# Weight loads of the down projection's block products issued four units ahead instead of five

## The chip, the cores and the metric

The kernel runs on one core of a Trainium2 chip. The metric is the device time of one execution in microseconds (us). The kernel before takes 2042.51 us, the median of three runs (2041.34 to 2043.54). The engines are TensorE (PE; its weight loads are PEld), VectorE (DVE), ScalarE (ACT), GpSimd (POOL) and SyncE (SP), which issues most DMAs.

## The reference

The program is a two-layer decoder trunk over 512 tokens of width 1024. Each layer is a SwiGLU FFN, a token mixer (a gated DeltaNet in layer 0, spatial gating in layer 1) and another FFN; so there are four FFNs. Only the FFN's last matrix product is touched by the change:

```
def swiglu(h, w_gate, w_up, w_down):
    return (jax.nn.silu(h @ w_gate) * (h @ w_up)) @ w_down      # D_FF = 2816, D_MODEL = 1024
x = x + 0.5 * rmsnorm(swiglu(rmsnorm(x, g0), w_gate, w_up, w_down), g1)
```

## The kernel before, in words

**Split operands.** Every fp32 operand is split into a rounded high part and a low part (`split`, line 106: a cast on ACT at L108, a subtraction on DVE at L110), and a product is three matmuls: high by high, high by low, low by high. A loaded weight tile thus costs one DMA on SP's queue, one ACT cast and one DVE subtraction.

**The down projection** (`down`, line 536) multiplies the gated activations (22 row blocks of 128, `m` before the split, `ms` after it) by `w_down`. Its result lies in eight PSUM banks `y`, two for each of the blocks (1,0), (0,0), (1,1) and (0,1). Row blocks 0 to 7 are not multiplied plainly: they are taken as a 2x2 block matrix in a scheme with seven products instead of eight. Its products are named a11, s1, s2, a12, s3, a22 and s4. Each has two halves (q = 0, 1), and each half needs a weight tile `dw` (24 matmuls of 512 columns per product); the first half brings the activations `dm` too. For s1, s2, a12 and s3 VectorE first builds sums of weight blocks (`dsum`) or of activations (`dts`). `load_down` (line 472) issues all of that: the DMAs into `raw` (a ring of four buffers), the sums, the casts and the subtractions.

**One bank, several products.** a11, s2, s3 and a22 add up in the same two banks, block (1,0). After a11, after s2 and after s3 the running sum has to be kept: `keep` (line 574) copies both banks to a tile `dk` on ACT (L579). The next product of that block adds to the same banks, so TensorE may not begin it before the copy.

**The order of the work.** `ORDER` interleaves the products with four plain row blocks (8 to 11), whose matmuls go to the blocks (0,0) and (1,1) first:

```
ORDER = ("a11", 8, "s1", 9, "s2", 10, "a12", 11, "s3", "a22", "s4")
def ahead(self, n):
    while sum(c for _, c in self.ready) < n and self.queue:
        load, cost = self.queue.pop(0)
        self.ready.append((load(), cost))

def wget(self, n=1):
    self.ahead(n)
    out = [self.ready.pop(0)[0] for _ in range(n)]
    self.ahead(self.depth)
    return out
```

A unit is one half of a product or one plain row block. `wget` hands out the next unit and then issues loads until `depth` units stand ready, before the matmuls of the unit that it handed out are written. `depth` is 3 in the rest of the kernel. `need` (line 700) splits the activations of the plain row blocks into `ms` when their turn comes. A scheduler then orders each engine's instructions and may move an instruction past others that it thinks not ready; each engine works its own list in order. Between the a11 halves stand two leftover steps of the gate and up projections (`pa`, `pc`, L400), the last of which is `p3`.

Of the kernel before, what the change touches and what calls it, by code (L numbers as in the profile page):

```python
# [27 lines left out]
class Trunk:  # L28
# [507 lines left out]
    def down(self, get, need, on_token, rest):  # L536

        nc = self.nc
        V = nc.vector
        d = {}  # L540
        for blk in ((1, 0), (0, 0), (1, 1), (0, 1)):
            d[blk] = [self.bank("y") for _ in range(2)]
        begun = set()
        rest = list(rest)

        def mm(blk, s, lhsT, rhs, stop=False):
            nc.tensor.matmul(d[blk][s], lhsT, rhs, start=(blk, s) not in begun, stop=stop, skip_group_check=True)  # L547
            begun.add((blk, s))

        def product(blk):  # L550
            m = None
            for q in range(2):
                (w, mq), = self.wget()
                m = mq or m
                for s in range(2):
                    for j in range(2):
                        l = [m[:, i, q * 2 + j, s * P:(s + 1) * P] for i in range(2)]
                        for a, b in ((0, 0), (0, 1), (1, 0)):
                            mm(blk, s, l[a], w[:, b, j])
                if rest:  # L560
                    rest.pop(0)()
            self.tick()

        def plain(kt, wt, blks, stop=False):
            for blk in blks:
                i, k = blk
                for s in range(2):
                    m = get(kt, 2 * k + s)
                    for a, b in ((0, 0), (0, 1), (1, 0)):
                        mm(blk, s, m[a], wt[b][:, i * 512:(i + 1) * 512], stop and a == 1)  # L570

        keeps = {}

        def keep(blk, n):
            if n != 2:
                keeps["t"] = self.big([P, 2, 2, 512], F32, name="dk")
            k = keeps[n] = keeps["t"][:, 0 if n != 2 else 1]
            for s in range(2):
                nc.scalar.copy(out=k[:, s], in_=d[blk][s])  # L579

        def add(out, blk, k):
            for s in range(2):
                V.tensor_tensor(out=d[blk][s] if out is None else out[:, s], in0=d[blk][s], in1=k[:, s], op=ALU.add)

        self.depth = 5
        held = []
        for n in self.ORDER:
            if isinstance(n, int):
                need(n)
                wt, = self.wget()  # L590
                plain(n, wt, ((0, 0), (1, 1)))
                held.append((n, wt))
                self.tick()
                continue
            if n == "s3":
                add(None, (0, 0), keeps[1])
            product({"a12": (0, 0), "s1": (0, 1), "s4": (0, 1)}.get(n, (1, 0)))
            if n in ("a11", "s2", "s3"):
                keep((1, 0), {"a11": 1, "s2": 2, "s3": 3}[n])
            if n == "s3":  # L600
                add(keeps[3], (0, 1), keeps[3])
                add(None, (1, 1), keeps[3])
        self.depth = 3
        on_token.prepare()
        add(None, (0, 1), keeps[2])
        for blk in ((1, 0), (0, 1)):
            for kt, wt in held:
                plain(kt, wt, (blk,))
            self.tick()
        for kt in range(12, NF - 5):  # L610
            need(kt)
            wt, = self.wget()
            plain(kt, wt, ((0, 0), (1, 0), (0, 1), (1, 1)))
            self.tick()
        need(NF - 1)
        tail = self.wget(5)
        for t in range(NT):
            for hfs in (((0, 1),) if t < NT - 1 else ((0,), (1,))):
                for i, kt in enumerate(range(NF - 5, NF)):
                    m = get(kt, t)  # L620
                    for a, b in ((0, 0), (0, 1), (1, 0)):
                        for hf in hfs:
                            mm((hf, t // 2), t % 2, m[a], tail[i][b][:, hf * 512:(hf + 1) * 512], kt == NF - 1 and a == 1)
                    if i == 1 and hfs[0] == 0:
                        self.tick()
            on_token(t, d[(0, t // 2)][t % 2], d[(1, t // 2)][t % 2])
            self.tick()
# [1008 lines left out]
```

## Time and profile before

| | us |
|---|---|
| median of three runs | 2042.51 |
| the profiled execution | 2040.34 |
| its span, first to last instruction | 2038.6 |
| TensorE busy in it | 1986.3 |
| TensorE idle until a `dk` copy, four times | 21.0 |
| mean granted TensorE clock | 0.992 of full speed |

The profile is one execution. The span is what lies between the first and the last instruction, and 1.74 us lie around it. TensorE is busy for 97% of it, so a reader looks for the stretches in which it isn't, or in which its clock is lower. The four down projections begin at 247, 925, 1275 and 1906 us.

### The profile page before, as it was taken

How to read it: one execution, taken by the hardware profiler on the slowest of the kernel's cores; microseconds unless marked ns; L12 is line 12 of the kernel's file. 1: busy time of each engine (PE TensorE's matmuls, PEld its weight loads, DVE VectorE, ACT ScalarE, POOL GpSimd, SP SyncE). 2: the span in 40 equal slices, each digit the busy share in tenths (PEclk: the TensorE clock that was granted, in tenths of full speed). 3: DMA queues.
4: the chain of work that ended last, by engine and by line, in shares of the span. 5: the costliest groups of instructions: out<-in, count | busy, mean ns of one | idle time of the engine just before them, and what ended most of it. 6: DMA issues, size and time to landing. Idle time of an engine off the chain costs nothing.

```text
span 2038.6 us, 32697 instructions
## 1 busy us (share of the span) xinstructions
PE 1986.3 (97%) x13418; PEld 1804.3 (89%) x13418; DVE 1436.0 (70%) x2006; ACT 966.4 (47%) x1688; POOL 131.6 (6%) x202
## 2 busy tenths in 40 slices
PE   7999989999998999998999999899999999999898
PEld 7999978988877899997889999788888889999887
DVE  6787793777946688888568887947455529888862
ACT  5455552585435555555345555534223426555451
POOL 1000000111135100000010000001000000000000
PEclk9999999999999999999999999999999999999999
DMA  5333364244221433335522333553322613333451
GB/s 166 94 111 107 117 204 145 85 142 125 92 74 68 141 94 104 108 112 183 208 73 90 110 113 115 181 196 133 99 84 83 228 51 96 112 102 106 153 188 42
DMA packets 172424, 246.45 MB, mean 121 GB/s; under 512 B 19257, under 2 KB 131185, under 8 KB 169842
## 3 DMA queue, kind: packets, MB, share of 16 engines
q1 hardware_dynamic: 162946, 212.68, 33.7%
q10 hardware_dynamic: 9328, 31.68, 4.0%
q8 instruction: 105, 1.72, 0.4%
q14 instruction: 45, 0.37, 0.1%
HBM read 230.12 MB, written 14.21 MB: 120 GB/s over the span
## 4 chain that ended last, share of the span: by engine, by line
PE 63%; DVE 3%; issue 1%; ACT 1%; POOL 0%; DMA 0%; ACTq 0%; DVEq 0%; POOLq 0%
PE pa L400 17%; PE y L547 15%; PE pc L400 8%; PE y L334 6%; PE pb L400 4%; PE pu L201 2%; PE pu L200 2%; PE pu L199 2%; PE pv L199 1%; PE pv L201 1%; PE pv L200 1%; PE px L1467 1%; DVE dw L110 1%; PE pg L200 0%; PE pg L201 0%
## 5 line engine op out<-in xcount | busy, mean ns | idle before, releaser
L547 PE MATMUL y<-w,ms 128*128 128x512 f32 x1344 | 315.7, 395 | 0.0
L547 PEld LDWEIGHTS y<-w,ms 128*128 128x128 f32 x1344 | 255.6, 191 | 54.6 <-DVE ms L110 1.5
L400 PE MATMUL pa<-hsh,ws 128*128 128x256 f32 x1248 | 250.1, 283 | 0.0
L108 ACT CAST ws<-wsum 128x1024 fp32r<-128x1024 f32 x156 | 161.8, 1051 | 117.8 <-DVE wsum L170 100.8
L400 PEld LDWEIGHTS pa<-hsh,ws 128*128 128x128 f32 x1248 | 206.1, 192 | 0.0
L110 DVE TENSOR_TENSOR w<-raw,w 128x1024 fp32r<-128x1024 f32 x154 | 186.0, 1225 | 24.7 <-ACT w L108 23.9
L110 DVE TENSOR_TENSOR ws<-wsum,ws 128x1024 fp32r<-128x1024 f32 x156 | 189.5, 1222 | 10.6 <-ACT ws L108 9.2
L547 PE MATMUL y<-dw,dm 128*128 128x512 f32 x672 | 161.2, 396 | 21.1 <-ACT dk L579 21.0
L108 ACT CAST w<-raw 128x1024 fp32r<-128x1024 f32 x155 | 158.5, 1049 | 40.8 <-DMA raw<-in_sg_w_out 6.7
L400 PE MATMUL pa<-hsl,ws 128*128 128x256 f32 x624 | 176.9, 283 | 0.0
L547 PEld LDWEIGHTS y<-dw,dm 128*128 128x128 f32 x672 | 126.5, 190 | 49.5 <-ACT dk L579 22.3
L408 ACT COPY keep<-pa 128x256 f32<-128x256 f32 x234 | 86.5, 370 | 146.5 <-PE pa L400 144.2
L311 DVE TENSOR_TENSOR bt<-y,gain 128x512 f32<-128x512 f32 x48 | 32.7, 689 | 156.0 <-ACT junk L307 155.5
L400 PE MATMUL pa<-hq,wa 128*128 128x256 f32 x936 | 125.4, 283 | 0.0
L400 PE MATMUL pb<-hq,wa 128*128 128x256 f32 x936 | 125.1, 283 | 0.0
L400 PE MATMUL pc<-hsh,ws 128*128 128x256 f32 x624 | 125.1, 283 | 0.0
L400 PE MATMUL pa<-hsh,wd 128*128 128x256 f32 x624 | 125.0, 283 | 0.0
L400 PE MATMUL pc<-hq,ws 128*128 128x256 f32 x936 | 125.0, 283 | 0.0
L400 PEld LDWEIGHTS pa<-hsl,ws 128*128 128x128 f32 x624 | 119.9, 192 | 0.0
L400 PEld LDWEIGHTS pc<-hq,ws 128*128 128x128 f32 x936 | 118.2, 192 | 0.3
L400 PEld LDWEIGHTS pa<-hq,wa 128*128 128x128 f32 x936 | 118.1, 192 | 0.0
L400 PEld LDWEIGHTS pb<-hq,wa 128*128 128x128 f32 x936 | 118.0, 192 | 0.0
(328 smaller groups left out, 4306.7 us busy)
## 6 DMA issues: line engine op xcount, KB each, us to landing
raw<-in_ffn_w_down SPq DMA_DIRECT2D x120, 512.0 KB, 4.3
raw<-in_ffn_w_gate SPq DMA_DIRECT2D x88, 512.0 KB, 3.8
raw<-in_ffn_w_up SPq DMA_DIRECT2D x88, 512.0 KB, 4.1
raw<-in_dn_w_in SPq DMA_DIRECT2D x32, 512.0 KB, 4.5
raw<-in_sg_w_in SPq DMA_DIRECT2D x32, 512.0 KB, 4.4
xs<-x ACTq DMA_DIRECT2D x20, 512.0 KB, 2.6
x<-xs ACTq DMA_DIRECT2D x10, 1024.0 KB, 10.1
raw<-in_sg_w_out SPq DMA_DIRECT2D x16, 512.0 KB, 4.5
```

The lines of the kernel that those rows point to most:

```text
L108: self.nc.scalar.copy(out=hi, in_=src)
L110: e.tensor_tensor(out=lo, in0=src, in1=hi.bitcast(F32), op=ALU.subtract)
L199: nc.tensor.matmul(out, lhsT[0], rhs[0], start=start, stop=False)
L200: nc.tensor.matmul(out, lhsT[0], rhs[1], start=False, stop=False)
L201: nc.tensor.matmul(out, lhsT[1], rhs[0], start=False, stop=stop)
L311: nc.vector.tensor_tensor(out=tmp[:, c], in0=y, in1=grow[:, c], op=ALU.mult)
L334: self.nc.tensor.matmul(y[t][hf], m[a], wt[b][:, hf * 512:(hf + 1) * 512], start=(kt == 0 and a == 0 and b == 0), stop=(kt == nk - 1 and a ...
L400: nc.tensor.matmul(out, wts[w][x][:, k], t[y][:, k], start=(first and k == 0 and m == 0), stop=(k == 3 and m == 2), skip_group_check=not f ...
L408: nc.scalar.copy(out=kept[n], in_=ba)
L547: nc.tensor.matmul(d[blk][s], lhsT, rhs, start=(blk, s) not in begun, stop=stop, skip_group_check=True)
L1467: nc.tensor.matmul(px[:, n * P:(n + 1) * P], self.v[c // 4][:, n, c % 4 * P:(c % 4 + 1) * P], self.wt[:, cp], start=True, stop=True)
```

## The change

The number of units that stand ready ahead while the block products run becomes four. Nothing else is edited.

```
@@ -582,7 +582,7 @@
             for s in range(2):
                 V.tensor_tensor(out=d[blk][s] if out is None else out[:, s], in0=d[blk][s], in1=k[:, s], op=ALU.add)
 
-        self.depth = 5
+        self.depth = 4
         held = []
         for n in self.ORDER:
             if isinstance(n, int):
```

Before, when the second half of a11 was handed out, the first half of s2 (five units on) was loaded at once, ahead of the copies that follow a11. Now the loads then stop at row block 9, and the first half of s2 is loaded when row block 8 is handed out, after `need(8)`.

On ACT, in the fourth down projection, from the cast of row block 9's weights to the second `ms` cast, this stood before (`dk_18877` is the copy after a11, `y_18783` and `y_18784` are the banks of block (1,0), `dw_18844` and `dm_18848` belong to s2, `ms_18880` to row block 8):

```order
L108 CAST w_18813<-raw_18811 128x1024 [waits DMAHW3_49]
L108 CAST dw_18844<-dsum_18664 128x1024 [waits DVE_49,PE_49]
L108 CAST dm_18848<-dts_18670 128x1024 [waits DVE_49,PE_49]
L579 COPY dk_18877<-y_18783 128x512 [waits PE_49]
L579 COPY dk_18877<-y_18784 128x512 [waits PE_49]
L108 CAST ms_18880<-m_17053 128x1024
L108 CAST ms_18883<-m_17053 128x1024
```

and this stands now (`dk_18867` is the copy, `ms_18870` row block 8, `dw_18879` and `dm_18883` s2):

```order
L108 CAST w_18838<-raw_18836 128x1024 [waits DMAHW3_49]
L579 COPY dk_18867<-y_18783 128x512 [waits PE_49]
L579 COPY dk_18867<-y_18784 128x512 [waits PE_49]
L108 CAST ms_18870<-m_17053 128x1024
L108 CAST ms_18873<-m_17053 128x1024
L108 CAST dw_18879<-dsum_18664 128x1024 [waits DVE_49]
L108 CAST dm_18883<-dts_18670 128x1024 [waits DVE_49]
```

The two casts of s2 have moved from before the copies to behind the two `ms` casts. On TensorE, at the same place, from p3 (`pc`) to the first matmuls of s1 (`dw_18796`), this stood before:

```order
L400 MATMUL pc_18699<-hq_15845,ws_18560 128x256 x12
L547 MATMUL y_18783<-dw_18844,dm_18848 128x512 x3
L547 MATMUL y_18785<-w_18681,ms_18880 128x512 x2
L547 MATMUL y_18786<-w_18681,ms_18880 128x512
L547 MATMUL y_18785<-w_18681,ms_18880 128x512
L547 MATMUL y_18786<-w_18681,ms_18880 128x512 x2
L547 MATMUL y_18787<-w_18681,ms_18880 128x512 x3
L547 MATMUL y_18788<-w_18681,ms_18880 128x512 x3
L547 MATMUL y_18789<-dw_18796,dm_18800 128x512 x6
```

and this stands now:

```order
L400 MATMUL pc_18699<-hq_15845,ws_18560 128x256 x12
L547 MATMUL y_18785<-w_18681,ms_18870 128x512 x2
L547 MATMUL y_18786<-w_18681,ms_18870 128x512 x2
L547 MATMUL y_18787<-w_18681,ms_18870 128x512 x2
L547 MATMUL y_18788<-w_18681,ms_18870 128x512 x2
L547 MATMUL y_18785<-w_18681,ms_18870 128x512
L547 MATMUL y_18786<-w_18681,ms_18870 128x512
L547 MATMUL y_18787<-w_18681,ms_18870 128x512
L547 MATMUL y_18788<-w_18681,ms_18870 128x512
L547 MATMUL y_18789<-dw_18796,dm_18800 128x512 x6
```

Three matmuls of s2 stood in front of row block 8; they are gone from there and stand with the other 21 of s2, behind row block 9. At the copies after s3 ACT had this before (`dw_19084` is the last half of s4, `w_19101` row block 12):

```order
L108 CAST dw_19084<-dsum_18664 128x1024 [waits DVE_49]
L108 CAST w_19101<-raw_19099 128x1024 [waits DMAHW0_49,PE_49]
L579 COPY dk_19116<-y_18783 128x512 [waits DVE_49,PE_49]
L579 COPY dk_19116<-y_18784 128x512 [waits PE_49]
L108 CAST w_19125<-raw_19123 128x1024
```

and has this now (`dw_19096` is the last half of s4, `w_19120` row block 12):

```order
L108 CAST dw_19096<-dsum_18664 128x1024 [waits DVE_49]
L579 COPY dk_19111<-y_18783 128x512 [waits PE_49]
L579 COPY dk_19111<-y_18784 128x512
L108 CAST w_19120<-raw_19118 128x1024 [waits DMAHW0_49]
```

The copies now precede row block 12's cast, and the second copy has no wait of its own any more: the first copy's wait on TensorE covers both banks. The order of the DMAs on SP's queue is the same in both programs.

## Rows read from the trace of the kernel before

**Rows 1.** The page: the span, and TensorE's share of it.
```profile
span 2038.6 us, 32697 instructions
PE 1986.3 (97%) x13418; PEld 1804.3 (89%) x13418; DVE 1436.0 (70%) x2006; ACT 966.4 (47%) x1688; POOL 131.6 (6%) x202
```

**Rows 2.** Waits of TensorE: us in total, times, longest us.
```profile
PE y L547 <- ACT dk L579: 21.0, 4, 5.2
```

**Rows 3.** Timeline, TensorE, fourth projection: start, us, what [idle before <-releaser].
```profile
1913.38 1.59 PE L400 MATMUL pc<-hq,ws 128*128 128x256 f32 x12
1920.22 1.78 PE L547 MATMUL y<-dw,dm 128*128 128x512 f32 x3 [5.25 <-ACT dk L579]
1921.80 4.93 PE L547 MATMUL y<-w,ms 128*128 128x512 f32 x12
1926.57 5.63 PE L547 MATMUL y<-dw,dm 128*128 128x512 f32 x24
...
1950.39 16.48 PE L547 MATMUL y<-dw,dm 128*128 128x512 f32 x72
1966.71 65.44 PE L547 MATMUL y<-w,ms 128*128 128x512 f32 x288
```

**Rows 4.** Timeline, TensorE, the same place in down projections one to three.
```profile
260.82 1.78 PE L547 MATMUL y<-dw,dm 128*128 128x512 f32 x3 [5.25 <-ACT dk L579]
...
265.86 5.61 PE L547 MATMUL y<-dw,dm 128*128 128x512 f32 x24
...
938.30 1.78 PE L547 MATMUL y<-dw,dm 128*128 128x512 f32 x3 [5.25 <-ACT dk L579]
...
944.15 5.62 PE L547 MATMUL y<-dw,dm 128*128 128x512 f32 x24
...
1289.13 1.78 PE L547 MATMUL y<-dw,dm 128*128 128x512 f32 x3 [5.24 <-ACT dk L579]
...
1295.32 5.61 PE L547 MATMUL y<-dw,dm 128*128 128x512 f32 x24
```

**Rows 5.** Timeline, ACT, the same place in the fourth down projection.
```profile
1913.35 1.04 ACT L108 CAST w<-raw 128x1024 fp32r<-128x1024 f32 x1
...
1917.50 1.04 ACT L108 CAST dw<-dsum 128x1024 fp32r<-128x1024 f32 x1 [3.11 <-DVE dsum L494]
...
1919.59 1.07 ACT L579 COPY dk<-y 128x512 f32<-128x512 f32 x2
...
1920.54 2.00 ACT L108 CAST ms<-m 128x1024 fp32r<-128x1024 f32 x2
```

**Rows 6.** Busy time by stretch: A:B, us, engines, granted clock, DMA share, GB/s.
```profile
1919.00:1920.00 1.00, 0.00 (x0) 0.00 (x0) 1.00 (x2) 1.00 (x2) 0.00 (x0) 0.65 0.71 227
...
1925.50:1926.00 0.50, 0.50 (x2) 0.40 (x2) 0.50 (x1) 0.50 (x1) 0.00 (x0) 0.50 0.00 0
```

**Rows 7.** Timeline, DVE, fourth down projection: bank additions and subtractions that follow each other.
```profile
1952.04 1.29 DVE L583 TENSOR_TENSOR y<-y,dk 128x512 f32<-128x512 f32 x2
...
1959.34 3.48 DVE L110 TENSOR_TENSOR w<-raw,w 128x1024 fp32r<-128x1024 f32 x3
```

**Rows 8.** Timeline, DVE, second down projection, the sum for s3's second half.
```profile
960.06 1.23 DVE L501 TENSOR_TENSOR raw<-raw,raw 128x1024 f32<-128x1024 f32 x1 [1.94 <-DMA raw<-in_ffn_w_down]
```

**Rows 9.** Timeline, ACT, the copies after s3 in the fourth down projection.
```profile
1954.67 0.59 ACT L579 COPY dk<-y 128x512 f32<-128x512 f32 x1 [0.30 <-PE y L547]
1956.03 0.59 ACT L579 COPY dk<-y 128x512 f32<-128x512 f32 x1 [0.77 <-PE y L547]
```

**Rows 10.** Timeline, TensorE, two other waits, in the DeltaNet.
```profile
597.86 4.75 PE L1220 MATMUL pw<-ninv,kb 128*128 128x128 f32 x24 [2.31 <-DVE kb L1216]
...
649.01 1.09 PE L1293 MATMUL po<-vn,ea 64*64 64x128 f32 x16 [1.54 <-DVE vn L1275]
```

**Rows 11.** Busy time by stretch around the waits of the group above.
```profile
645.00:650.00 5.00, 3.46 (x40) 2.54 (x34) 3.92 (x5) 0.28 (x1) 1.61 (x1) 1.00 1.00 372
...
598.00:602.00 4.00, 3.94 (x20) 3.68 (x21) 2.71 (x2) 0.97 (x2) 4.00 (x4) 0.57 0.29 114
```

More of the change, by code (lines that the diff above doesn't have):

```diff
@@ L583, in add @@
                 V.tensor_tensor(out=d[blk][s] if out is None else out[:, s], in0=d[blk][s], in1=k[:, s], op=ALU.add)
-        self.depth = 5
+        self.depth = 4
         held = []
```

## The prediction

> **What bounds the kernel now.** I read the page first: TensorE is busy for 1986.3 of 2038.6 us [rows 1], so only its idle time, or time at a lower clock, can be won. The waits of TensorE come next. One kind stands out: four waits for a `dk` copy on ACT, 21.0 us in all, 5.2 us the longest [rows 2]. One lies in each down projection, at the same place: before three matmuls of s2, which need the copy after a11 [rows 3, 4]. Then the timeline of ACT at that place, to see why the copy is late. p3 ends on TensorE at 1913.38 + 1.59 = 1914.97 [rows 3] and a11 before it, so the copy could have begun then. ACT, however, works its list in order, and before the copies stand the casts of s2's first half. The first of them idles 3.11 us until VectorE has built the sum, at 1917.50; the copies begin only at 1919.59 [rows 5]. Last, the granted clock: it is 0.65 between 1919 and 1920 and still 0.50 (1.2 GHz) just before 1926 [rows 6], after TensorE had done nothing from 1914.97 to 1920.22. So the matmuls behind the wait pay too: row block 8's 12 take 4.93 us, where 72 in a row take 1966.71 - 1950.39 = 16.32 us, or 0.227 each [rows 3].
>
> The place as a whole, from the end of p3 to the start of s1, is 1926.57 - 1914.97 = 11.60 us in the fourth projection [rows 3]. In the others the end of p3 is the start of the three matmuls less their wait [rows 4]: 265.86 - 255.57 = 10.29, 944.15 - 933.05 = 11.10, and 1295.32 - 1283.89 = 11.43.
>
> **The change, part by part.** *Moved: the load of s2's first half.* It is one DMA, two VectorE sums (`dsum`, `dts`), two ACT casts and two VectorE subtractions, now written behind the copies and behind the casts for row block 8. SP's order is the same in both programs, and its DMA waits for a free buffer of the ring, so it is issued as before. No work is removed or added; what changes is who stands before whom.
>
> *The new place on ACT.* Row block 9's cast ends at 1913.35 + 1.04 = 1914.39. The copy pair takes 1920.54 - 1919.59 = 0.95 us of ACT's list, one `ms` cast about 1.05 (two took 2.00) [rows 5], so the high part of `ms` is there at 1916.39. In the trace the first matmul came 0.2 us after that cast (1920.54 + 1.05 to 1921.80) [rows 3, 5]. So row block 8, which now stands first in TensorE's list, begins at 1916.6: TensorE waits 1.63 us instead of 5.25. Its 12 matmuls take 12 x 0.227 = 2.72 us, if the clock holds. The last four need the low part, one VectorE operation behind the high part (3.48 / 3 = 1.16 us [rows 7], so about 1917.6); the first eight last until 1918.4. s1 then begins at 1919.32, 4.35 us from p3's end. The three matmuls of s2 are done later, 0.68 us, so 5.03 us stand against 11.60.
>
> The gains are 11.60 - 5.03 = 6.57 us in the fourth, and 5.26, 6.07 and 6.40 in the first three: 24.3 us.
>
> *The cover that was taken away.* s2's operands now come later, and each later product's behind them. I take VectorE's list there as gapless, at 1.16 us an operation and 0.65 for a short one (a bank addition, 1.29 / 2) [rows 7]. Behind the subtraction of `ms` (1917.6) stand one short product, then a second `ms` subtraction, two `dsum` sums, a `dts` sum and s2's first two subtractions: 0.65 + 6 x 1.16, so 1925.2. TensorE reaches s2 at 1919.32 + 36 x 0.227 = 1927.5 (s1 and row block 9 lie between). That is 2.3 us of slack. To s3, VectorE has 14 more operations (1941.4) and TensorE 72 matmuls (1943.8): 2.4 us. The second half of s3 needs another sum, two bank additions and a subtraction, 1945.0 against 1946.5: 1.5 us. So I cost this at nothing, with that slack as the cover. The bounds are 0 and, where the cover goes, the wait of 1.94 us for a DMA that VectorE shows at just this sum in the second projection [rows 8], passed on to TensorE twice in each projection: 15.5 us.
>
> *The copies after s3.* The order shows that the first copy's wait now covers both banks, so it waits for s3's last matmul, where before it needed only the first bank's. In the trace s3 ended at 1950.39 + 24 x 0.227 = 1955.83, and the first copy began at 1954.67, 0.2 us after its bank's last matmul, which lay six matmuls before that end; a22 followed without a wait [rows 3, 9]. Now the first copy begins at the end plus 0.2, takes 0.59 [rows 9], and TensorE follows 0.04 later (first copy 1919.59 + 0.59, matmul 1920.22) [rows 3, 5]: a new wait of 0.83 us, 3.3 us in four. It is 0 if the copy still goes with its bank, and 0.2 + 2 x 0.59 = 1.4 us (5.5 in four) if both copies count. I take 3.3, the rows' own account.
>
> *Also moved:* row block 12's cast goes behind the copies after s3. It is needed only after a22, s4 and 48 more matmuls, 96 x 0.227 = 22 us later, so it costs nothing.
>
> **The sum.** 24.3 - 3.3 = 21.0 us. Against the profiled execution's own 2040.34 us (span 2038.6, 1.74 around it) that is 2019.3. The median of the runs lies 2.2 us above this execution; 2042.5 - 21.0 gives **2021.5 us**, which I forecast. Nothing between the projections should eat it: TensorE is the busy engine there too, and a stage that begins earlier has its weights asked for earlier as well.
>
> **The rivals.**
>
> *The clock falls all the same.* Two short waits stand where one long one stood. The clock's price is what the place loses beyond the wait: from the three matmuls to s1 is 6.35 us for 15 x 0.227 = 3.40 of work in the fourth projection [rows 3], so 2.95; by the same account 1.64, 2.45 and 2.79 in the others [rows 4], 9.8 in all (some of it is the wait for `ms` from VectorE). The gain would be 21.0 - 9.8 = 11.2, the time 2031.3. For it: a wait of 2.31 us was followed by a clock of 0.57. Against it: a single wait of 1.54 us left the clock at 1.00 [rows 10, 11], and the new waits are 1.63 and 0.83 us, some 30 us apart. The Trainium skill's page "TensorE: Matmul & The Clock Gate", section "A second HAM failure mode: psum-queue depth-cycling", says that frequent short idles of TensorE between groups of matmuls make its clock swing between its two levels and cost throughput. By that rule the time would be nearer to 2031; the stretch with the 1.54 us wait speaks against it here, the one with 2.31 for it.
>
> *Late operands.* One unit less of lead lets a new wait take the old one's place, in s2 or s3, for weights, sums or subtractions. At the upper bound above, 15.5 us, the gain is 5.5 and the time 2037; at half of that, which is likelier since the slack has to go first, 2029. For it: VectorE's full list, and rows 8. Against: the slack of 1.5 to 2.4 us at each place.
>
> *The new copy wait doesn't appear*, since the first bank's release is seen earlier: 24.3 us, 2018.2.
>
> *Slower.* The shallower lead makes TensorE wait at every half of a product and every row block from row block 8 to s4, since each cast and subtraction arrives just after it is needed. These are 16 units in each projection, 64 in all, and the change turns slower from 24.3 / 64 = 0.38 us a unit; at 0.5 us the time is 2042.5 + 32 - 24.3 = 2050. Against it: two VectorE operations of 1.16 us a unit keep up with TensorE's 12 x 0.227 = 2.72 us, and few units need more than two.
>
> *The change does nothing:* the waits turn up at the same copies for another reason, such as a late cast of row block 9 before them on ACT. The order leaves nothing else before them that could be late: time unchanged.
>
> **How the numbers follow.** Forecast 0.66, clock 0.10, late operands 0.14, no new copy wait 0.04, slower 0.04, nothing 0.02. About 0.2% of the time, 4 us, is what a measurement of this kernel can tell from no change. Forecast, clock, no copy wait and nearly all of late operands lie beyond it: faster 0.93. The case of nothing and the rim of late operands make same 0.03; slower has 0.04. The likeliest case's own range is 2018 to 2025. For 8 in 10 I go to 2016 below (the copy wait absent and a little more) and to 2029 above, which takes in half of the late operands and leaves out the clock.
>
> **What the profile of the changed kernel would show.** If the steps hold, the 21.0 us of waits for a `dk` copy become about 3 us, four of about 0.8 before a22; four waits of about 1.6 us for an `ms` cast appear before row block 8; the granted clock stays at 1.00 from p3 on, and row block 8's 12 matmuls take 2.7 to 2.9 us; from p3's end to s1 lie about 4.4 us. The forecast is wrong if the clock is 0.50 behind the 1.6 us wait, if TensorE waits for `dw` or `dm` in s2 or s3, or if the wait for `ms` is over 3 us, because ACT's list held up the copies.

## The result, and the profile after

The changed kernel takes 2020.36 us, the median of four runs (2019.19 to 2020.97), against 2041.95 for the kernel before on the same chip. The ratio is 0.9891, 95% interval 0.9878 to 0.9905, so about 22 us are gained; 2021.5 was forecast. The profiled execution took 2019.86 us. Its page begins:

```profile
span 2018.1 us, 32685 instructions
PE 1977.1 (98%) x13418; PEld 1797.9 (89%) x13418; DVE 1434.3 (71%) x2006; ACT 966.9 (48%) x1688; POOL 132.5 (7%) x202
```

Against [rows 1] the span is 20.5 us shorter. TensorE is busy for 9.2 us less with the same instructions, mostly those behind the old wait, which then ran at the lower clock; its idle time (span less busy) has shrunk from 52.3 to 41.0 us. The waits of TensorE in the block products, in the columns of [rows 2]:

```profile
PE y L547 <- ACT ms L108: 5.9, 4, 1.8
...
PE y L547 <- ACT dk L579: 2.7, 4, 0.7
```

The 21.0 us for a `dk` copy have become 5.9 for an `ms` cast and 2.7 for a copy at another place, 8.6 in all. The timeline of TensorE in the fourth down projection, from p3 to the products after s3, answers to [rows 3]:

```profile
1898.59 1.59 PE L400 MATMUL pc<-hq,ws 128*128 128x256 f32 x12
...
1901.56 3.01 PE L547 MATMUL y<-w,ms 128*128 128x512 f32 x12 [1.38 <-ACT ms L108]
1904.41 5.60 PE L547 MATMUL y<-dw,dm 128*128 128x512 f32 x24
...
1912.57 5.60 PE L547 MATMUL y<-dw,dm 128*128 128x512 f32 x24
...
1928.89 5.60 PE L547 MATMUL y<-dw,dm 128*128 128x512 f32 x24
1935.17 11.18 PE L547 MATMUL y<-dw,dm 128*128 128x512 f32 x48 [0.68 <-ACT dk L579]
```

In both traces p3 runs behind the second half of a11, not between the halves. Row block 8 now follows p3, after 1.38 us instead of 5.25. Its 12 matmuls take 3.01 us, not 4.93, and s1 begins at 1904.41. s2 (1912.57) and s3 (1928.89) wait for nothing. The last row is a22 and s4, held 0.68 us by the copies after s3. ACT at the same place, beside [rows 5]:

```profile
1898.55 1.05 ACT L108 CAST w<-raw 128x1024 fp32r<-128x1024 f32 x1
1899.50 1.06 ACT L579 COPY dk<-y 128x512 f32<-128x512 f32 x2
1900.45 2.00 ACT L108 CAST ms<-m 128x1024 fp32r<-128x1024 f32 x2
1905.86 1.06 ACT L108 CAST dw<-dsum 128x1024 fp32r<-128x1024 f32 x1 [3.40 <-DVE dsum L494]
```

s2's first cast still idles ACT for over 3 us until VectorE has built its sum, but the copies and both `ms` casts are done by then: nothing that TensorE needs soon stands behind it. Last, the clock (columns as in [rows 6]) over the first new wait, row block 8, and the stretch with the second wait:

```profile
1900.00:1901.50 1.50, 0.18 (x2) 0.00 (x0) 1.50 (x3) 1.50 (x4) 0.00 (x0) 1.00 0.96 388
1901.50:1904.50 3.00, 2.94 (x13) 2.45 (x14) 3.00 (x4) 0.96 (x2) 0.00 (x0) 1.00 0.52 182
...
1934.00:1946.00 12.00, 11.32 (x51) 9.04 (x50) 10.20 (x12) 6.12 (x8) 0.00 (x0) 1.00 0.67 217
```

It stays at 1.00, 2.4 GHz, through both.

### The profile page after: what moved, and what is told of

Same layout as the page of the kernel before. It is cut to its first block, busy times and chain, and to the rows that moved or that the text cites. A ratio compares the mean times of both kernels' runs of the same rounds, so it can differ in the third digit from the quotient of the medians.

```text
span 2018.1 us, 32685 instructions
## 1 busy us (share of the span) xinstructions
PE 1977.1 (98%) x13418; PEld 1797.9 (89%) x13418; DVE 1434.3 (71%) x2006; ACT 966.9 (48%) x1688; POOL 132.5 (7%) x202
## 4 chain that ended last, share of the span: by engine, by line
PE 64%; DVE 1%; ACT 1%; issue 1%; DMA 1%; POOL 0%; ACTq 0%; DVEq 0%; POOLq 0%
PE pa L400 17%; PE y L547 16%; PE pc L400 8%; PE y L334 5%; PE pb L400 4%; PE pu L201 2%; PE pu L200 2%; PE pu L199 2%; PE pv L199 1%; PE pv L200 1%; PE pv L201 1%; PE px L1467 1%; PE pg L200 1%; PE pg L201 0%; PE pg L199 0%
## 5 line engine op out<-in xcount | busy, mean ns | idle before, releaser
L547 PE MATMUL y<-w,ms 128*128 128x512 f32 x1344 | 310.1, 390 | 5.9 <-ACT ms L108 5.9
L547 PEld LDWEIGHTS y<-w,ms 128*128 128x128 f32 x1344 | 251.5, 188 | 58.6 <-ACT ms L108 6.7
```

## The experiments

My theory: the gain comes from the order after a11. What TensorE needs first (the copies, then row block 8's `ms` casts) has to stand ahead of s2's operands, whose sums are late on VectorE, on every engine's list. Rivals: a shorter lead pays everywhere; the clock alone is the gain; the copies alone matter; ACT's list alone matters.

**One half of the change at a time.** First, four units until a11 has been handed out and five from there on:

```
             product(...)
+            if n == "a11":
+                self.depth = 5
```

> Lead of four units until a11 is handed out, five from there on: the first half of the change alone. Order on ACT (theory 1: the gain comes from the copies and the ms casts standing ahead of s2's casts after a11): nearly all of the gain stays, four waits for an ms cast of 1 to 3 us before row block 8, no wait for a dk copy over 1 us, time 2020 to 2030 (the late s2 load could follow sooner and put a wait of up to 1.3 us before row block 12, about 2.4 us a projection more than with four throughout). A shorter lead as such (theory 2: fewer units under way leave VectorE and ACT less crowded everywhere): half of the gain, about 2031. The clock (theory 3: the gain is what the clock lost behind the wait) expects the clock at 1.00 and the full gain, 2020.

Measured: 2021.37 us, ratio 0.9895 (0.9878 to 0.9911). Nearly all of the gain is there. The waits in the block products:

```profile
PE y L547 <- ACT ms L108: 5.5, 4, 1.4
PE y L547 <- ACT w L108: 4.5, 4, 1.1
```

The second kind is new: row block 12's cast now waits for s3's last matmul, ahead of the copies after s3, and two of that row block's matmuls stand before a22 on TensorE. Then the reverse, five units through a11 (`if n == "a11": self.depth = 4` behind it):

> Lead of five units through a11, four from there on: the other half of the change alone. Theory 1 (order on ACT after a11): nothing is gained, since s2's casts stand before the copies as in the kernel before; the four waits for a dk copy are 5 to 7.5 us, row block 8 follows late, time 2042 to 2050. Theory 2 (a shorter lead as such): half of the gain, about 2031.

Measured: 2041.13 us, ratio 0.9996 (0.9986 to 1.0005): nothing gained. The wait at the place is the old one, not longer as I had allowed:

```profile
PE y L547 <- ACT dk L579: 21.0, 4, 5.2
```

So the lead pays at one place, a11, and a shorter lead as such is ruled out.

**The idle time filled.** The kernel before (a lead of five), with matmuls that nobody reads in the old wait; `last` holds the operands of the product just written:

```
+                last[:] = [w, m]
...
+            if n == "a11":
+                for _ in range(20):
+                    nc.tensor.matmul(d[(0, 0)][0], last[1][:, 0, 0, :P], last[0][:, 0, 0], start=True, ...)
```

> Lead of five units as in the kernel before, with 20 matmuls of work that nobody reads (20 x 0.227 = 4.54 us) put into the stretch in which TensorE waited for the copy, and six matmuls of s2 instead of three behind them. It takes away the idle time that the clock saw and leaves the operands as late as before. Theory 3 (the gain is mostly the clock): row block 8 at 0.227 us a matmul, clock 1.00 through s1, time 2020 to 2025. Theory 1 (the gain is mostly the wait itself): only the clock's part is won back, at most the 9.8 us that the matmuls behind the wait lost, time 2032 to 2040, and three to four us from p3's end to s1 beyond what the changed kernel needs.

Measured: 2033.83 us against 2042.71, ratio 0.9956 (0.9941 to 0.9971), 8.9 us less than before (5.9 to 12.1). The timeline of TensorE, first projection:

```profile
255.49 4.72 PE L603 MATMUL y<-dw,dm 128*128 128x512 f32 x20
260.90 1.72 PE L547 MATMUL y<-dw,dm 128*128 128x512 f32 x6 [0.68 <-ACT dk L582]
```

and the fourth:

```profile
1915.38 1.71 PE L547 MATMUL y<-dw,dm 128*128 128x512 f32 x6 [1.28 <-ACT dk L582]
1916.92 2.90 PE L547 MATMUL y<-w,ms 128*128 128x512 f32 x12
```

The 20 matmuls take 20 x 0.227 = 4.54 us, and in three projections 0.68 are still waited: the copy comes as late as before, but row block 8 takes 2.90 us in the fourth instead of 4.93. (The 1.28 us there are longer because row block 9's cast on ACT had itself waited 1.12 us for a DMA. Six matmuls of s2 now stand before row block 8, not three.) That separates the two costs of the old wait: about 8.9 us by the clock, and the rest, some 13 of 22 (10 to 16 by the interval), by the idle time itself. The waits agree: from 21.0 to 8.6 us they lost 12.4. The clock alone is not the gain.

**The copies alone.** During a11 (`hold`) no load beyond four units; the fifth (s2's first half) is issued between the copies and `need(8)`:

```
+                self.depth = 4 if hold and q else 5
...
+            if n == "a11":
+                self.depth = 5
+                self.ahead(5)
```

> Lead of five units, but during a11 no load further ahead than four is issued; after a11's copies have been issued the lead is filled up to five, before row block 8. So the copies stand before s2's casts, as in the changed kernel, but the ms casts stand behind those casts, as in the kernel before, and two matmuls of s2 stand before row block 8 on TensorE. Theory 1a (the copies standing in front of s2's casts is all that matters): most of the gain is there, 2020 to 2026. Theory 1b (what matters is that everything row block 8 needs, the ms casts too, stands in front of s2's casts, and row block 8 in front of s2 on TensorE): nothing is gained; the wait at this place turns from a wait for dk into one for the dm cast or subtraction of s2, 6 to 9 us, time 2042 to 2062.

Measured: 2043.20 us, ratio 1.0008 (0.9998 to 1.0018). The timeline of ACT, fourth projection:

```profile
1918.72 1.05 ACT L580 COPY dk<-y 128x512 f32<-128x512 f32 x2
1922.20 1.05 ACT L108 CAST dw<-dsum 128x1024 fp32r<-128x1024 f32 x1 [2.43 <-DVE dsum L494]
1923.94 1.05 ACT L108 CAST dm<-dts 128x1024 fp32r<-128x1024 f32 x1 [0.69 <-DVE dts L520]
1924.89 1.99 ACT L108 CAST ms<-m 128x1024 fp32r<-128x1024 f32 x2
```

and of TensorE:

```profile
1925.04 1.22 PE L547 MATMUL y<-dw,dm 128*128 128x512 f32 x2 [5.65 <-ACT dm L108]
1926.06 4.71 PE L547 MATMUL y<-w,ms 128*128 128x512 f32 x12
```

The copies are there over 5 us before s2's matmuls, and nothing is won: the `dm` cast of s2 takes their place as the releaser, two of s2's matmuls stand first on TensorE, and the `ms` casts are as late as before. So the name in the waits of before (`dk`) was only the last of a list that was late as a whole. Whether the `ms` casts on ACT or the matmuls of s2 ahead of row block 8 on TensorE would hold it up by themselves isn't shown: no run moved one without the other.

**ACT's list alone.** Lead of five, with the copies after a11 (`n == 1` in `keep`) on VectorE:

```
-                nc.scalar.copy(out=k[:, s], in_=d[blk][s])
+                if n == 1:
+                    V.tensor_copy(k[:, s], d[blk][s])
+                else:
+                    nc.scalar.copy(out=k[:, s], in_=d[blk][s])
```

> Lead of five units as in the kernel before, but the copies after a11 (4 pairs in the kernel) are made by VectorE instead of ACT, so that they stand behind no cast of ACT's list; the rest of the order is the one that the planner makes of it. Order theory: the wait for dk after a11 goes or falls below 2 us; the copies take 0.6 us each of VectorE's list, and the ms casts become the limit, with a wait of 1.4 to 2 us before row block 8; time 2020 to 2030. Rival (VectorE's list is the real limit, ACT only passes its lateness on): the wait stays at 4 us or more, with VectorE as the releaser, time 2036 to 2045.

Measured: 2050.22 us, ratio 1.0043 (1.0028 to 1.0058): slower. What the order theory expected, a wait below 2 us, failed; the rival named beside it, VectorE's list as the real limit, had the releaser right and a time too low. The waits of TensorE, and VectorE's timeline in the fourth projection:

```profile
PE y L547 <- DVE dk L580: 30.1, 4, 7.5
```

```profile
1924.84 1.23 DVE L494 TENSOR_TENSOR dsum<-dsum,raw 128x1024 f32<-128x1024 f32 x1
1925.97 1.23 DVE L520 TENSOR_TENSOR dts<-m,dts 128x1024 f32<-128x1024 f32 x1
...
1928.57 1.23 DVE L110 TENSOR_TENSOR dm<-dts,dm 128x1024 fp32r<-128x1024 f32 x1
...
1930.31 1.29 DVE L580 COPY dk<-y 128x512 f32<-128x512 f32 x2
```

VectorE works its list in order too. On it the copies stand behind s2's sums and even its subtractions, which on ACT they did not, so the wait is 7.53 us instead of 5.25. Moving the copy to another engine at the same place in the program doesn't help here. The lateness itself comes from VectorE's list: ACT's list passes it on, when the copies stand behind casts that wait for VectorE's sums.

**The lead, step by step** (`self.depth = 6`, `3`, `2` and `1`). Six:

> Lead of six units throughout: one more cast (the second half of s2, whose sum is one VectorE operation later again) stands before the copies after a11. Order theory: the copies come about 1.1 us later than with five, the wait for dk is 6.3 to 6.6 us instead of 5.25, the matmuls behind it lose as much to the clock, time 2046 to 2050. Lead as such (each unit of lead costs as much as the fifth did): 2063. Rival in which only the fifth unit matters and later ones change nothing: 2042.

Measured: 2046.58 us, ratio 1.0024 (1.0013 to 1.0035), and the wait has grown by one cast to 6.38 us, as the order theory has it:

```profile
PE y L547 <- ACT dk L579: 25.5, 4, 6.4
```

Three:

> Lead of three units throughout. Theory 1: row block 9's cast goes behind the copies too, so the copies and the ms cast come about 1 us sooner; the waits for an ms cast fall from 1.4 to about 0.6 us, the one for a dk copy after s3 stays at 0.7, nothing else waits, and the time is 1.2 us a projection below that with four, 2015 to 2016. Rival (the operands' slack of 1.5 to 2.4 us at s2 and s3 is used up): new waits for dw or dm of s2 and s3, 1 to 2 us each, time 2022 to 2035. Theory 2 expects another gain of the size of the first, 2000.

Measured: 2014.75 us, ratio 0.9863 (0.9848 to 0.9878). Row block 9's cast is gone from before the copies; the operands of s2 and s3 still come in time. The wait after s3 has shrunk too, which I had not expected:

```profile
PE y L547 <- ACT ms L108: 1.7, 4, 0.4
...
PE y L547 <- ACT dk L579: 0.9, 4, 0.2
```

Two:

> Lead of two units throughout. With three the waits for an ms cast are 0.4 us and those for the dk copy after s3 0.2, 2.6 us in all over the four projections, at a median of 2014.75. Order theory: both waits go, and s2 and s3 still have their operands in time, since VectorE's list keeps the same order of sums: 2.6 us less, 2012. Late operands (the shorter lead must at some point put a sum or a subtraction behind its matmul): new waits for dw, dm or ms, from 0.5 us in each unit, time over 2020.

Measured: 2010.01 us, ratio 0.9847 (0.9832 to 0.9861). TensorE has no wait left in the block products. The fourth projection, p3 to s1:

```profile
1891.46 1.59 PE L400 MATMUL pc<-hq,ws 128*128 128x256 f32 x12
1892.90 2.96 PE L547 MATMUL y<-w,ms 128*128 128x512 f32 x12
1895.70 5.60 PE L547 MATMUL y<-dw,dm 128*128 128x512 f32 x24
```

One:

> Lead of one unit throughout, to find where a shorter lead turns. The first half of s1 now goes behind the copies and the ms casts too, with its two sums and its two subtractions on VectorE; between p3's end and s1 TensorE has only row block 8's 12 matmuls, 2.72 us. Order theory with VectorE's list as its limit: no wait before row block 8, but a wait of 3 to 6 us for dw or dm of s1, and the clock falls behind it as in the kernel before; time 2022 to 2040. Theory that a shorter lead as such is better: again some microseconds less than with two, 2006.

Measured: 2038.64 us, ratio 0.9983 (0.9973 to 0.9992): nearly all of the gain is gone. The waits, TensorE's timeline and the windows, all as above:

```profile
PE y L547 <- ACT dm L108: 15.7, 4, 4.1
```

```profile
1913.09 2.94 PE L547 MATMUL y<-w,ms 128*128 128x512 f32 x12
1919.89 1.19 PE L547 MATMUL y<-dw,dm 128*128 128x512 f32 x4 [3.87 <-ACT dm L108]
...
1922.57 7.32 PE L547 MATMUL y<-dw,dm 128*128 128x512 f32 x20
```

```profile
1915.90:1919.80 3.90, 0.13 (x1) 0.00 (x0) 3.90 (x4) 1.00 (x1) 0.00 (x0) 1.00 0.68 246
1919.80:1920.90 1.10, 1.01 (x4) 0.67 (x4) 1.10 (x2) 1.01 (x3) 0.00 (x0) 1.00 0.00 0
1920.90:1922.00 1.10, 0.21 (x2) 0.02 (x1) 1.10 (x2) 1.10 (x3) 0.00 (x0) 0.68 0.75 190
1922.00:1926.00 4.00, 4.00 (x10) 3.18 (x11) 4.00 (x5) 0.87 (x1) 0.00 (x0) 0.50 0.93 332
```

Now s1's sums and subtractions stand between and behind the two `ms` subtractions on VectorE, and only row block 8, 2.72 us, covers them. The rival on late operands, wrong for the change, is right three steps further.

**The best version beside the changed one**, on one chip:

> The changed kernel once more, beside the next one on the same chip: 2019 to 2021.

> Lead of two units once more: if its time holds, 2009 to 2012, 8 to 11 us below the changed kernel beside it, of which the four waits for ms and four for dk that it takes away (5.9 + 2.7 = 8.6 us) are the most.

Measured: 2019.24 us with four (ratio 0.9890, 0.9875 to 0.9905) and 2009.57 with two (0.9842, 0.9827 to 0.9857). The lead of two is 9.7 us faster; the waits that it takes away make 8.6 of them (8.4 in this profile of four). The rest is within the spread of the runs.

## Why the prediction was right, point by point

*The gain at the place.* From p3's end to s1 4.35 us were worked out; measured are 4.23, 4.25, 4.63 and 4.23 (fourth: 1904.41 - 1898.59 - 1.59). With 0.68 for the three moved matmuls the gains are 5.38, 6.17, 6.12 and 6.69, together 24.4 us where 24.3 stood. The third misses because its wait was 1.76, not 1.38: there row block 9's cast, ahead of the copies on ACT, had waited for its DMA. That the sums agree to 0.1 us is partly luck. The other waits were 0.25 us shorter than worked out, but row block 8 then took 2.85 us until s1 and not 2.72, and the third projection's 0.28 us of loss cancels the small gains of the rest.

*The wait for `ms`.* 1.63 was expected, 1.38 three times and 1.76 once measured. The chain from row block 9's cast to TensorE took 1901.56 - 1898.55 = 3.01 us in the fourth, where 1.04 + 0.95 + 1.05 + 0.2 = 3.24 had been added up. Instructions that follow each other on ACT overlap by some 0.1 us in the rows (the cast ends at 1898.55 + 1.05 = 1899.60, the copies begin at 1899.50). And the 0.2 us from the `ms` cast to TensorE was misread: in [rows 3] three matmuls of s2 still kept TensorE busy until row block 8 began. Here, where nothing stands between, it follows 1901.56 - (1900.45 + 1.05) = 0.06 us after the cast, if the first of the two casts takes 1.05.

*The new copy wait.* 0.83 us each was the term. The trace shows 0.68 idle, and 1935.17 - (1928.89 + 24 x 0.227) = 0.83 between s3's computed end and a22. Neither half of the change alone has it: with five units through a11 nothing waits there, with five behind a11 it is row block 12's cast. In the first of these two kernels the cast of row block 12 stands between the two copies, and the first copy begins at 1954.69, before s3 ends (1950.41 + 24 x 0.227 = 1955.86). So it goes with the order of ACT's list, as the term assumed.

*The slack on VectorE.* Three figures were 2.3, 2.4 and 1.5 us. Its rows after, the subtractions for s2's first half and for s3's two halves:

```profile
1909.15 1.22 DVE L110 TENSOR_TENSOR dm<-dts,dm 128x1024 fp32r<-128x1024 f32 x1
...
1925.05 1.22 DVE L110 TENSOR_TENSOR dm<-dts,dm 128x1024 fp32r<-128x1024 f32 x1
...
1928.53 2.36 DVE L110 TENSOR_TENSOR dw<-raw,dw 128x1024 fp32r<-128x1024 f32 x2
```

They end at 1910.37, 1926.27 and 1929.7 (half of the last group); TensorE comes at 1912.57, 1928.89 and 1928.89 + 12 x 0.227 = 1931.61. The slack is 2.2, 2.6 and 1.9 us, and cost nothing, as taken.

*The clock.* It stayed at 1.00, so the rival of 2031 fell. Its price in the kernel before was put at 9.8 us; the filled wait measured 8.9 (5.9 to 12.1). The Trainium skill's page "TensorE: Matmul & The Clock Gate", section "A second HAM failure mode: psum-queue depth-cycling", has the clock swing under frequent short idles; two waits of 0.7 to 1.8 us a projection did not make it do so here.

*The sum.* 21.0 us were forecast; the span lost 20.5, the median 21.6. a11 begins at 920.45 in the second projection, where it began at 924.54: of the 5.38 us of the first, less 0.83 for the copy, 4.1 have arrived, some 0.4 less than they should be. The DeltaNet lies between, and in it TensorE's wait for `kb` was 4.7 us in six parts, against 3.9 in four:

```profile
PE pw L1220 <- DVE kb L1216: 4.7, 6, 2.3
```

The changed kernel's second profile has 3.9 in four again, and a11 begins there at 920.18, so this belongs to the execution and not to the change.

What the prediction missed was not in the sum: it worked out VectorE's slack at four units and did not ask how far a smaller lead could go. At two, where the time is 10 us lower, the same subtractions stand so:

```profile
1902.06 1.22 DVE L110 TENSOR_TENSOR dm<-dts,dm 128x1024 fp32r<-128x1024 f32 x1
...
1917.95 1.23 DVE L110 TENSOR_TENSOR dm<-dts,dm 128x1024 fp32r<-128x1024 f32 x1
...
1921.62 2.36 DVE L110 TENSOR_TENSOR dw<-raw,dw 128x1024 fp32r<-128x1024 f32 x2
```

TensorE begins s2 at 1903.86 and s3 at 1920.18, so 0.6, 1.0 and 0.1 us of slack are left: two works, but only just.

## What to carry to other kernels

In a list worked in order, an early prefetch isn't free: whatever is issued ahead stands in front of the next urgent instruction, and if its own input is late, it makes that one late too. Put what the busiest engine needs first ahead of the prefetches that wait for late inputs. Here moving the copies alone, or moving them to another engine, only changed the name in the waits. The lead had an optimum: 2046.58 us with six, 2020.36 with four, 2014.75 with three, 2010.01 with two and 2038.64 with one. It turned where VectorE's slack ran out, so work that slack out and try both sides.

## What the runs showed of the hardware

The clock can fall after TensorE has resumed. In the fourth projection of the kernel with a lead of one it is still at 1.00 over the 3.87 us wait and the 1.1 us of work behind it, falls to 0.50 (1.2 GHz) in the next 1.1 us, in which TensorE waits 0.89 us for a cast, and 20 matmuls then take 7.32 us instead of 20 x 0.227 + 0.16 = 4.70. In the first projection of the same execution a wait of the same length has its price at once, and the four matmuls behind it take 1.96 us instead of 1.19:

```profile
262.26 1.96 PE L547 MATMUL y<-dw,dm 128*128 128x512 f32 x4 [3.87 <-ACT dm L108]
```

In the kernel before it fell within the 5.25 us wait itself [rows 6]. The waits of 1.38 to 1.76 us in the changed kernel left it at 1.00. So the length of the wait alone doesn't tell, here, when the price is paid. With matmuls that nobody reads in the old wait the clock stayed at 1.00, and row block 8 took 2.90 us.
